# Up-projection with its long and short products in runs of their own, and gate maxima broadcast by DMA instead of by TensorE

## The chip, the cores and the metric

The kernel runs on one core of a Trainium2 chip. The metric is the device time of one execution, in microseconds (us). A core has TensorE (PE, with the weight loads shown as PEld), VectorE (DVE), ScalarE (ACT), GpSimd (POOL) and SyncE (SP, which issues most DMAs). Each engine works through its own instructions in order; semaphores hold an instruction until what it needs is there.

## The reference

One layer of a hybrid block for 256 tokens, width 2048. The parts that matter here are the gates of the chunkwise mLSTM (4 heads, chunks of 128 tokens) and the up-projection of the convolutional feed-forward net:

```python
h = rmsnorm(x, norm1_g[l])
proj = h @ w_in[l]
...
# mLSTM, in each chunk of 128 tokens
b = jnp.cumsum(lf, axis=-1)
dmat = jnp.where(tril, b[..., :, None] - b[..., None, :] + li[..., None, :], -jnp.inf)
inter = b + m_st[..., None]
m_t = jnp.maximum(jnp.max(dmat, axis=-1), inter)
w_in = jnp.exp(dmat - m_t[..., None])
p = jnp.einsum('bhtd,bhsd->bhts', qc, kc) * w_in
...
x = x + y @ w_out[l]
h = rmsnorm(x, norm2_g[l])
u = causal_dwconv(h @ w_up[l], ffn_conv_w[l], ffn_conv_b[l])
u_g, u_v = jnp.split(u, 2, axis=-1)
x = x + (jax.nn.silu(u_g) * u_v) @ w_down[l]
```

`w_up` is 2048 x 11264, `w_down` 5632 x 2048.

## The kernel before

**Weights.** Every weight matrix is streamed once, in chunks of 1 MB. `load_chunk` reads a chunk with one SyncE DMA into `raw` (3 buffers), and for each half of it ScalarE casts the high part `whi` (line 90) and VectorE subtracts to get the low part `wlo` (line 91). Of each there are 4 buffers, one half each, so two chunks. A product with full accuracy is the sum of high times high, high times low and low times high. These steps are given a priority 100 instructions ahead, and a scheduler orders all engines but TensorE by simulated readiness; TensorE keeps the order in which the code is written.

**Stages on TensorE.** First `f_group` (short products of 256 columns, lines 131 to 133: weights stationary, activations `x` moving) for parts of the query and key projections; then `mixer` for each of four heads, made of `t_block` (long products of 512 columns, lines 112 to 114: activations stationary, weights moving), with two more `f_group` stretches in between; then `t_block` for the output projection `w_out`, with the stationary tiles `yh` and `yl`; then the up-projection `wide_group` (lines 610 to 626); then the down-projection (lines 672 to 674, long products).

**Small work in between.** `Slots` counts half chunks: `slots.after(n, fn)` runs `fn` after n of them, so that the gates, the mLSTM and the attention stand between the big products. `gates()` makes rows of 4 heads: `mx`, the running maxima (line 374 completes it). Before, they are split in `mh` and `ml`, and `mlstm` copies row j to all 128 partitions with two products by `selr` and adds the causal mask with a third by `identr`, into the PSUM tile `pm`; ScalarE takes the exponentials from there (line 420). The weights `ptm`, `pth`, `ptl` of the values follow on VectorE and ScalarE, and two half chunks later TensorE multiplies them with the values (lines 437 to 440). The tile `gb` (a gain row, broadcast by a GpSimd DMA) takes over the buffer of `mx`.

**Up-projection.** 22 groups (11 for the gate half into the PSUM tiles `acc`, 11 for the value half into `side`), each of 4 chunks (512 rows of `w_up` by 512 columns). For each of 4 row blocks k and 4 column blocks f there is a pair: a long product, `whi` with the high and low parts of the activations side by side (512 columns), and a short one, `wlo` with the high part alone (256 columns). `spread2` puts four small products into the first group. Behind each group VectorE and ScalarE do the convolution (`ffn_conv`, lines 300 to 308 and 635, 636).

Of the kernel before, what the change touches and what calls it, by code (L numbers as in the profile page):

```python
# [11 lines left out]
F32 = mybir.dt.float32  # L12
F32R = mybir.dt.float32r
AF = mybir.ActivationFunctionType
ALU = mybir.AluOpType
AX = mybir.AxisListType

P = 128
S = 256
# [43 lines left out]
def block_kernel(ctx: ExitStack, tc, x, xT, w_in, ifb, qkw, mg, qg, kg, dl, sg, w_out,  # L63
# [12 lines left out]
    def side():  # L76
        return psum.tile([P, 512], F32, tag="side", name="side")
# [135 lines left out]
    def row_norm(ssq, name):  # L213
# [6 lines left out]
        def spread():  # L220
            ps = side()
            for t in range(2):
# [3 lines left out]
            nc.vector.tensor_copy(rsb, ps[:, :S])  # L226
        return rs, rsb, spread

    sel = start.tile([AH, AH, P], F32, name="sel")
    nc.gpsimd.memset(sel, 0.0)  # L230
    nc.gpsimd.affine_select(sel, sel, pattern=[[-1, AH], [0, P]], compare_op=ALU.not_equal,
                            fill=1.0, base=0, channel_multiplier=1)
    cmask = start.tile([P, P], F32, name="cmask")
    nc.gpsimd.memset(cmask, 0.0)
    nc.gpsimd.affine_select(cmask, cmask, pattern=[[1, P]], compare_op=ALU.is_ge,
                            fill=BIG, base=0, channel_multiplier=-1)
    selr = const.tile([AH, AH, P], F32R, name="selr")
    nc.scalar.copy(selr, sel)
    cmr = const.tile([P, 2, P], F32R, name="cmr")
    nc.scalar.copy(cmr, cmask.unsqueeze(1).broadcast_to([P, 2, P]))  # L240
    identr = const.tile([P, P], F32R, name="identr")
    nc.scalar.copy(identr, ident)

    ifr = const.tile([P, KT, 36], F32, name="ifr")
    nc.gpsimd.memset(ifr, 0.0)
    for n in range(2):
# [81 lines left out]
    def gates():  # L328
# [10 lines left out]
        def rows():  # L339
            ps = side()  # L340
            for k in range(KT):
                a, b = hh[k // 4][:, k % 4], hl[k // 4][:, k % 4]
                w = ws[k // 8][:, k % 8]
                nc.tensor.matmul(ps[:100, :S], w, a, start=k == 0, stop=k == KT - 1, skip_group_check=True)
                nc.tensor.matmul(ps[:36, :S], w[:, :36], b, start=False, stop=k == KT - 1, skip_group_check=True)
            rows4 = pa.tile([AH, 4, S], F32, tag="qn", name="rows4")
            li, f, e, lf = (rows4[:, n] for n in range(4))
            for n, r in enumerate((li, f)):
                nc.scalar.copy(r, ps[64 + 32 * n:64 + 32 * n + AH, :S])
                nc.vector.tensor_tensor(r, ps[32 * n:32 * n + AH, :S], r, ALU.add)  # L350
                nc.vector.tensor_tensor(r, r, rsb1[:AH], ALU.mult)
                nc.vector.tensor_scalar_add(r, r, ib[:, n:n + 1])

            nc.scalar.activation(e, f, AF.Abs)
            nc.scalar.activation(e, e, AF.Exp, scale=-1.0)
            nc.scalar.activation(e, e, AF.Ln, bias=1.0)
            nc.vector.scalar_tensor_tensor(lf, f, 0.0, e, ALU.min, ALU.subtract)

            rows3 = pa.tile([AH, 2 * S + S + P], F32, tag="yb", name="rows3")
            b, nm, a = rows3[:, :S], rows3[:, S:2 * S], rows3[:, 2 * S:]  # L360
            mx = pa.tile([AH, S + P], F32, tag="gb", name="mx", bufs=1)
            for c in range(2):
                cs = slice(c * P, (c + 1) * P)
                nc.vector.tensor_tensor_scan(b[:, cs], ones[:AH, :], lf[:, cs], 0.0, ALU.mult, ALU.add)
            nc.vector.tensor_tensor(a[:, :S], li, b, ALU.subtract)

            nc.vector.tensor_scalar_add(a[:, S:], a[:, :P], b[:, P - 1:P])
            nc.vector.tensor_tensor_scan(mx[:, :P], a[:, :P], a[:, :P], 0.0, ALU.max, ALU.max)
            m1 = pa.tile([AH, 1], F32, name="m1")
            nc.vector.tensor_tensor(m1, b[:, P - 1:P], mx[:, P - 1:P], ALU.add)  # L370
            nc.vector.tensor_tensor_scan(mx[:, P:S], a[:, P:S], a[:, P:S], m1, ALU.max, ALU.max)
            nc.vector.scalar_tensor_tensor(nm, b, -1.0, mx[:, :S], ALU.mult, ALU.subtract)
            nc.vector.tensor_scalar_min(nm, nm, 88.0)
            nc.vector.tensor_copy(mx[:, S:], mx[:, P:S])
            mh = pa.tile([AH, S + P], F32R, name="mh")
            nc.scalar.copy(mh, mx)
            ml = pa.tile([AH, S + P], F32R, name="ml")
            nc.vector.tensor_tensor(ml, mx, mh.bitcast(F32), ALU.subtract)
            gate["mx"] = mh, ml

            def cols():
                pc = side()
                for n, src in enumerate((a[:, :P], a[:, P:S], a[:, S:], nm[:, :P], nm[:, P:])):
                    nc.tensor.transpose(pc[:, n * AH:(n + 1) * AH], src, ident[:AH, :AH])
                ac = pa.tile([P, 3, AH], F32, name="ac")
                em = pa.tile([P, 2, AH], F32, name="em")
                nc.vector.tensor_copy(ac, pc[:, :3 * AH].rearrange("p (n h) -> p n h", h=AH))
                nc.scalar.activation(em, pc[:, 3 * AH:5 * AH].rearrange("p (n h) -> p n h", h=AH), AF.Exp)
                gate["ac"], gate["em"] = ac, em
            slots.after(8, cols)  # L390
# [11 lines left out]
    def mlstm(j, v, hm):  # L402
# [1 line left out]
        gb = pa.tile([P, AV], F32, tag="gb", name="gb", bufs=1)  # L404
        nc.gpsimd.dma_start(gb, mg[:, j * AV:(j + 1) * AV].partition_broadcast(P))
        q, k = qk[j], qk[AH + j]
        pm, pq = side(), side()
        kw = dict(skip_group_check=True)

        for n, mx in enumerate(gate["mx"]):  # L410
            nc.tensor.matmul(pm[:, :3 * P], selr[:, j], mx, start=n == 0, stop=False, **kw)
        nc.tensor.matmul(pm[:, :S], identr, cmr.rearrange("p n s -> p (n s)"), start=False, stop=True, **kw)
        first = pq.rearrange("p (n s) -> p n s", s=S)[:, :, :P]
        for d in range(2):
            nc.tensor.matmul(first, k[:, d, :P], q[:, d], start=d == 0, stop=False, **kw)
# [1 line left out]
        w = pa.tile([P, 3 * P], F32, tag="wt", name="wt", bufs=1)  # L417
        ac = gate["ac"]
        for n in range(3):
            nc.scalar.activation(w[:, n * P:(n + 1) * P], pm[:, n * P:(n + 1) * P], AF.Exp,  # L420
                                 scale=-1.0, bias=ac[:, n, j:j + 1])
        pt = pa.tile([P, 3 * P], F32, tag="ptm", name="ptm", bufs=1)
        nc.vector.scalar_tensor_tensor(pt, pq[:, :3 * P], AQK ** -0.5, w, ALU.mult, ALU.mult)
# [186 lines left out]
    def wide_group(w, col, bank):  # L610


        ps = [bank() for _ in range(4)]
        for c in range(4):
            parts = col_chunk(w, c, col)
            for i in range(2):
                for k in (2 * i, 2 * i + 1):
                    first, last = c == 0 and k == 0, c == 3 and k == 3
                    for f in range(4):
                        whi, wlo = (t[:, f * P:(f + 1) * P] for t in parts[k])  # L620
                        nc.tensor.matmul(ps[f], whi, z[c][:, k].rearrange("p t s -> p (t s)"),  # L621
                                         start=first, stop=last, skip_group_check=True)
                        nc.tensor.matmul(ps[f][:, :S], wlo, z[c][:, k, 0],  # L623
                                         start=False, stop=last, skip_group_check=True)
                slots.tick()
        return ps

# [92 lines left out]
```

## Time and profile before

| | |
|---|---|
| time, median of 3 runs (lowest, highest) | 1592.11 us (1583.66, 1592.16) |
| time of the profiled execution | 1592.0 us |
| its span | 1590.2 us |
| TensorE busy | 1579.3 us (99%) |
| weight loads on TensorE busy | 1340.8 us (84%) |
| VectorE busy | 1112.8 us (70%) |
| ScalarE busy | 827.8 us (52%) |
| GpSimd busy | 35.8 us (2%) |
| granted TensorE clock | 1.00 |
| DMA | 300.88 MB, 189 GB/s mean |

The time of an execution is a little longer than the span of its instructions. Matmuls overlap in the pipeline, so the duration of one on the page is longer than the distance to the next; the distance between starts, which the timeline gives, is what one costs in a stream.

### The profile page before, as it was taken

Reading aid. Unit: us, or ns where it says so; the run is one execution under the profiler, and the core shown is the slowest. Engines: PE = TensorE matmul, PEld = TensorE weight load, DVE = VectorE, ACT = ScalarE, POOL = GpSimd, SP = SyncE. Lnnn points to the kernel's source line nnn. Section 1 sums busy time; section 2 is a strip of 40 time slices with the busy share of each in tenths; the row PEclk is TensorE's granted clock in tenths of the full one; section 3 lists DMA queues with packets and bytes.
Section 4 is the critical chain, followed back from the end, with each engine's and each line's share of the span. In section 5 each row is a group of like instructions: output and inputs, shape, how many; then the busy total and the mean of one; then the engine's idle time right before and its main releaser. Section 6 shows DMA issues by size and latency. Waiting matters only on the chain.

```text
span 1590.2 us, 20513 instructions
## 1 busy us (share of the span) xinstructions
PE 1579.3 (99%) x8021; PEld 1340.8 (84%) x8021; DVE 1112.8 (70%) x1624; ACT 827.8 (52%) x1123; POOL 35.8 (2%) x54
## 2 busy tenths in 40 slices
PE   8999999999999999999999999999999999999998
PEld 8988888888988888888788888888888888888887
DVE  6868676876758757775798777667766776555554
ACT  6854545454554554455455555555555555444442
POOL 0000000000000000000000000000000000000000
PEclk9999999999999999999999999999999999999999
DMA  9656555554645555455655555555555555555553
GB/s 296 225 177 206 171 175 192 172 198 160 209 161 192 185 186 185 159 186 185 238 185 186 186 186 186 186 186 188 186 187 188 187 188 190 193 187 194 202 185 133
DMA packets 138554, 300.88 MB, mean 189 GB/s; under 512 B 9816, under 2 KB 12120, under 8 KB 132312
## 3 DMA queue, kind: packets, MB, share of 16 engines
q1 hardware_dynamic: 137720, 296.41, 55.3%
q10 hardware_dynamic: 416, 2.11, 0.4%
q0 software_dynamic: 320, 1.05, 0.3%
q8 instruction: 63, 1.03, 0.3%
q14 instruction: 35, 0.29, 0.0%
HBM read 297.44 MB, written 2.10 MB: 188 GB/s over the span
## 4 chain that ended last, share of the span: by engine, by line
PE 97%; DVE 1%; DMA 1%; SPq 0%; ACT 0%; issue 0%
PE acc L114 14%; PE acc L112 14%; PE acc L113 14%; PE side L621 10%; PE acc L621 10%; PE acc L623 5%; PE side L623 5%; PE side L674 3%; PE acc L674 3%; PE acc L673 3%; PE side L673 3%; PE acc L672 3%; PE side L672 3%; PE acc L133 2%; PE acc L132 2%; PE acc L131 2%
## 5 line engine op out<-in xcount | busy, mean ns | idle before, releaser
L91 DVE TENSOR_TENSOR wlo<-raw,whi 128x1024 fp32r<-128x1024 f32 x548 | 668.4, 1223 | 363.5 <-ACT whi L90 359.9
L90 ACT CAST whi<-raw 128x1024 fp32r<-128x1024 f32 x548 | 573.9, 1051 | 573.5 <-PE acc L114 234.5
L112 PE MATMUL acc<-whi,x 128*128 128x512 f32 x896 | 352.0, 393 | 0.0
L114 PE MATMUL acc<-whi,x 128*128 128x512 f32 x896 | 349.3, 390 | 0.0
L113 PE MATMUL acc<-wlo,x 128*128 128x512 f32 x896 | 349.0, 390 | 0.0
L621 PE MATMUL side<-x,whi 128*128 128x512 f32 x704 | 249.2, 399 | 0.0
L621 PE MATMUL acc<-x,whi 128*128 128x512 f32 x704 | 249.1, 398 | 0.0
L114 PEld LDWEIGHTS acc<-whi,x 128*128 128x128 f32 x896 | 168.1, 188 | 35.5
L623 PE MATMUL side<-x,wlo 128*128 128x256 f32 x704 | 197.7, 281 | 0.0
L623 PE MATMUL acc<-x,wlo 128*128 128x256 f32 x704 | 197.7, 281 | 0.0
L112 PEld LDWEIGHTS acc<-whi,x 128*128 128x128 f32 x896 | 168.3, 188 | 34.5
L113 PEld LDWEIGHTS acc<-wlo,x 128*128 128x128 f32 x896 | 168.3, 188 | 33.9
L621 PEld LDWEIGHTS side<-x,whi 128*128 128x128 f32 x704 | 132.3, 188 | 33.0
L621 PEld LDWEIGHTS acc<-x,whi 128*128 128x128 f32 x704 | 132.2, 188 | 32.7
L623 PEld LDWEIGHTS acc<-x,wlo 128*128 128x128 f32 x704 | 133.0, 189 | 0.0
L623 PEld LDWEIGHTS side<-x,wlo 128*128 128x128 f32 x704 | 133.0, 189 | 0.0
L308 DVE SCALAR_TENSOR_TENSOR cv<-tu,fwc,cv 128x256 f32<-128x256 f32 x176 | 73.3, 479 | 0.0
L673 PE MATMUL acc<-wlo,ah 128*128 128x512 f32 x176 | 68.5, 389 | 0.0
L672 PE MATMUL acc<-whi,ah 128*128 128x512 f32 x176 | 68.5, 389 | 0.0
L674 PE MATMUL acc<-whi,al 128*128 128x512 f32 x176 | 68.5, 389 | 0.0
L672 PE MATMUL side<-whi,ah 128*128 128x512 f32 x176 | 68.5, 389 | 0.0
L673 PE MATMUL side<-wlo,ah 128*128 128x512 f32 x176 | 68.5, 389 | 0.0
(207 smaller groups left out, 1727.0 us busy)
## 6 DMA issues: line engine op xcount, KB each, us to landing
raw<-w_in SPq DMA_DIRECT2D x126, 1024.0 KB, 5.0
raw<-w_up SPq DMA_DIRECT2D x88, 1024.0 KB, 5.1
raw<-w_down SPq DMA_DIRECT2D x44, 1024.0 KB, 4.8
raw<-w_out SPq DMA_DIRECT2D x16, 1024.0 KB, 5.1
wr<-w_in SPq DMA_DIRECT2D x8, 256.0 KB, 4.4
xs<-x SPq DMA_DIRECT2D x2, 1024.0 KB, 9.4
x<-x ACTq DMA_DIRECT2D x1, 2048.0 KB
out<-x SPq DMA_DIRECT2D x8, 256.0 KB, 2.4
```

The costliest lines, as they stand in the source:

```text
L90: nc.scalar.copy(hi, r)
L91: nc.vector.tensor_tensor(lo, r, hi.bitcast(F32), ALU.subtract)
L112: nc.tensor.matmul(ps[t], ah[c][:, k, tok], whi, start=first, stop=False)
L113: nc.tensor.matmul(ps[t], ah[c][:, k, tok], wlo, start=False, stop=False)
L114: nc.tensor.matmul(ps[t], al[c][:, k, tok], whi, start=False, stop=last)
L131: nc.tensor.matmul(o, whi, ah[c][:, k, :], start=st, stop=False, **kw)
L308: nc.vector.scalar_tensor_tensor(cv[:, f], tu[:, f, 3 - d:3 - d + S], wf[:, j:j + 1], cv[:, f], ALU.mult, ALU.add)
L621: nc.tensor.matmul(ps[f], whi, z[c][:, k].rearrange("p t s -> p (t s)"), start=first, stop=last, skip_group_check=True)
L623: nc.tensor.matmul(ps[f][:, :S], wlo, z[c][:, k, 0], start=False, stop=last, skip_group_check=True)
L672: nc.tensor.matmul(ps[n][t], h_, whi, start=k == 0, stop=False)
L673: nc.tensor.matmul(ps[n][t], h_, wlo, start=False, stop=False)
L674: nc.tensor.matmul(ps[n][t], l_, whi, start=False, stop=k == NFT - 1)
```

## The change

It has two parts. In `wide_group` the pairs are taken apart: in each chunk all 16 long products stand together and all 16 short ones, and the order of the two is reversed from chunk to chunk (`part = (c + i) % 2`), so that chunk 0 ends and chunk 1 begins with short ones, chunk 1 ends and chunk 2 begins with long ones. In the gates `mh`, `ml`, `selr`, `cmr` and `identr` are gone: GpSimd stores `mx` to DRAM, loads it back to all 128 partitions as `mxb`, and writes the causal mask into it with one `affine_select` per head; the exponentials read `mxb`.

```diff
-    sel = start.tile([AH, AH, P], F32, name="sel")
...
-    selr = const.tile([AH, AH, P], F32R, name="selr")
-    nc.scalar.copy(selr, sel)
-    cmr = const.tile([P, 2, P], F32R, name="cmr")
-    nc.scalar.copy(cmr, cmask.unsqueeze(1).broadcast_to([P, 2, P]))
-    identr = const.tile([P, P], F32R, name="identr")
-    nc.scalar.copy(identr, ident)
...
-            mh = pa.tile([AH, S + P], F32R, name="mh")
-            nc.scalar.copy(mh, mx)
-            ml = pa.tile([AH, S + P], F32R, name="ml")
-            nc.vector.tensor_tensor(ml, mx, mh.bitcast(F32), ALU.subtract)
-            gate["mx"] = mh, ml
+            mxd = tc.dram_tile([AH, S + P], F32, name="mxd")
+            nc.gpsimd.dma_start(mxd, mx)
+            mxb = pa.tile([P, AH, S + P], F32, name="mxb")
+            nc.gpsimd.dma_start(mxb, mxd.partition_broadcast(P))
+
+            for j in range(AH):
+                mj = mxb[:, j, :S].rearrange("p (n s) -> p n s", s=P)
+                nc.gpsimd.affine_select(mj, mj, pattern=[[0, 2], [1, P]], compare_op=ALU.is_ge,
+                                        fill=BIG, base=0, channel_multiplier=-1)
+            gate["mx"] = mxb
...
-        pm, pq = side(), side()
+        pq = side()
         kw = dict(skip_group_check=True)
 
-        for n, mx in enumerate(gate["mx"]):
-            nc.tensor.matmul(pm[:, :3 * P], selr[:, j], mx, start=n == 0, stop=False, **kw)
-        nc.tensor.matmul(pm[:, :S], identr, cmr.rearrange("p n s -> p (n s)"), start=False, stop=True, **kw)
...
-            nc.scalar.activation(w[:, n * P:(n + 1) * P], pm[:, n * P:(n + 1) * P], AF.Exp,
+            nc.scalar.activation(w[:, n * P:(n + 1) * P], gate["mx"][:, j, n * P:(n + 1) * P], AF.Exp,
...
             for i in range(2):
-                for k in (2 * i, 2 * i + 1):
-                    first, last = c == 0 and k == 0, c == 3 and k == 3
+                part = (c + i) % 2
+                for k in range(4):
                     for f in range(4):
-                        whi, wlo = (t[:, f * P:(f + 1) * P] for t in parts[k])
-                        nc.tensor.matmul(ps[f], whi, z[c][:, k].rearrange("p t s -> p (t s)"),
-                                         start=first, stop=last, skip_group_check=True)
-                        nc.tensor.matmul(ps[f][:, :S], wlo, z[c][:, k, 0],
-                                         start=False, stop=last, skip_group_check=True)
+                        wt = parts[k][part][:, f * P:(f + 1) * P]
+                        kw = dict(stop=c == 3 and k == 3, skip_group_check=True)
+                        if part == 0:
+                            nc.tensor.matmul(ps[f], wt, z[c][:, k].rearrange("p t s -> p (t s)"),
+                                             start=c == 0 and k == 0, **kw)
+                        else:
+                            nc.tensor.matmul(ps[f][:, :S], wt, z[c][:, k, 0], start=False, **kw)
                 slots.tick()
```

On TensorE, in the first group of the up-projection, the border of the first two chunks stood like this before (`x0` and `x1` are the activations of a chunk, the numbers tell buffers apart):

```order
L621 MATMUL acc_7171<-x0_6627,whi_7179 128x512
L623 MATMUL acc_7171<-x0_6627,wlo_7180 128x256
L621 MATMUL acc_7172<-x0_6627,whi_7179 128x512
L623 MATMUL acc_7172<-x0_6627,wlo_7180 128x256
L621 MATMUL acc_7169<-x1_6797,whi_7217 128x512
L623 MATMUL acc_7169<-x1_6797,wlo_7218 128x256
L621 MATMUL acc_7170<-x1_6797,whi_7217 128x512
L623 MATMUL acc_7170<-x1_6797,wlo_7218 128x256
```

And now the whole first group and the start of the second (16 equal rows are one row with x16; lines 612 and 615 are the long and the short product, line 225 is `spread2`):

```order
L612 MATMUL acc<-x_6609,whi 128x512 x16
L615 MATMUL acc<-x_6609,wlo 128x256 x16
L615 MATMUL acc<-x_6779,wlo 128x256 x16
L612 MATMUL acc<-x_6779,whi 128x512 x16
L612 MATMUL acc<-x_6949,whi 128x512 x16
L615 MATMUL acc<-x_6949,wlo 128x256 x16
L615 MATMUL acc<-x_7119,wlo 128x256 x16
L225 MATMUL side<-diag_7308,ones 128x128
L225 MATMUL side<-diag_7311,ones 128x128
L612 MATMUL acc<-x_7119,whi 128x512 x16
L612 MATMUL side<-x_6609,whi 128x512 x16
```

Long and short alternated from product to product; now they come in runs of 32 (16 at the very start), and a chunk's last high half is used at once with its first.

On ScalarE, around the exponentials of head 0, with the semaphores that each row waits for, it stood like this before:

```order
L388 ACTIVATE em<-side 128x8 [waits DVE_49]
L143 ACTIVATE vh<-acc,rs_577 128x512
L90 CAST whi<-raw 128x1024 [waits DMAHW3_49,PE_49,Activation_49]
L90 CAST whi<-raw 128x1024 [waits PE_49,Activation_49]
L420 ACTIVATE wt<-side,ac 128x128 [waits PE_49]
L420 ACTIVATE wt<-side,ac 128x128 x2
L425 CAST pth<-ptm 128x384 [waits DVE_49]
```

And now:

```order
L379 ACTIVATE em<-side 128x8 [waits DVE_49]
L143 ACTIVATE vh<-acc,rs_561 128x512
L90 CAST whi<-raw 128x1024 [waits DMAHW3_49,PE_49,Activation_49]
L408 ACTIVATE wt<-mxb,ac 128x128 [waits DMASW1_49,Pool_49]
L408 ACTIVATE wt<-mxb,ac 128x128 x2
L90 CAST whi<-raw 128x1024 [waits PE_49,Activation_49]
L413 CAST pth<-ptm 128x384 [waits DVE_49,Activation_49]
```

The exponentials moved ahead of one cast of weights, and they wait for GpSimd and its load (DMASW1) instead of for TensorE.

On GpSimd the mixers' first instructions stood like this before:

```order
L284 AFFINE_SELECT dist<-dist 128x256 [waits Pool_49]
L211 TENSOR_TENSOR rs_577<-rs_577,mhalf 128x2 [waits DVE_49]
L405 DMA gb<-mg 128x512 [waits DMAHW3_49,DMAHW4_49,DMAHW2_49,DMAHW5_49,DMAHW1_49,DMAHW6_49,DMAHW0_49,DMAHW7_49,DVE_49,PE_49]
L211 TENSOR_TENSOR mr<-mr,mhalf 128x1 [waits DVE_49] x2
L405 DMA gb<-mg 128x512 [waits DMASW0_49,DVE_49]
```

And now:

```order
L211 TENSOR_TENSOR rs_561<-rs_561,mhalf 128x2 [waits DVE_49]
L362 DMA mxd<-mx 4x384 [waits DMAHW3_49,DMAHW2_49,DMAHW4_49,DMAHW1_49,DMAHW5_49,DMAHW0_49,DMAHW6_49,DVE_49,DMAHW7_49,PE_49,Activation_49]
L364 DMA mxb<-mxd 128x1536 [waits DMASW0_49]
L396 DMA gb<-mg 128x512
L368 AFFINE_SELECT mxb<-mxb 128x256 [waits DMASW1_49]
L368 AFFINE_SELECT mxb<-mxb 128x256 x3
L211 TENSOR_TENSOR mr<-mr,mhalf 128x1 [waits DVE_49] x2
L396 DMA gb<-mg 128x512 [waits DMASW2_49,DVE_49]
```

The store, the load and four masks stand ahead of the first roots; the load waits for the store's landing (DMASW0), the masks for the load's.

## Rows read from the trace of the kernel before

**Rows 1.** The page: granted clock in 40 slices; chain that ended last, by engine.
```profile
PEclk9999999999999999999999999999999999999999
...
PE 97%; DVE 1%; DMA 1%; SPq 0%; ACT 0%; issue 0%
```

**Rows 2.** Timeline of TensorE, late up-projection (start, duration, engine, line); 33 pairs apart.
```profile
1000.00 0.40 PE L621 MATMUL acc<-x,whi 128*128 128x512 f32 x1
...
1011.66 0.40 PE L621 MATMUL side<-x,whi 128*128 128x512 f32 x1
```

**Rows 3.** Timeline of TensorE, early up-projection; 31 pairs apart.
```profile
854.94 0.39 PE L621 MATMUL acc<-x,whi 128*128 128x512 f32 x1
...
865.69 0.39 PE L621 MATMUL acc<-x,whi 128*128 128x512 f32 x1
```

**Rows 4.** Timeline of TensorE: the products of `spread2`.
```profile
867.77 0.61 PE L225 MATMUL side<-diag,ones 128*128 128x128 f32 x4
```

**Rows 5.** Line 621 on TensorE: count, duration (ns), first and last start.
```profile
L621 PE MATMUL acc<-x,whi x704: 391/398/481, 848.3 to 1322.9; 128*128 128x512 f32 x176
```

**Rows 6.** Timeline of TensorE, `f_group` (short products alone); 99 products apart.
```profile
20.04 0.28 PE L131 MATMUL acc<-x,whi 128*128 128x256 f32 x1
...
31.91 0.28 PE L131 MATMUL acc<-x,whi 128*128 128x256 f32 x1
```

**Rows 7.** Timeline of TensorE, down-projection (long products alone); 52 products apart.
```profile
1400.11 0.39 PE L674 MATMUL side<-whi,al 128*128 128x512 f32 x1
...
1411.90 0.39 PE L672 MATMUL acc<-whi,ah 128*128 128x512 f32 x1
```

**Rows 8.** Timeline of TensorE, output projection (long products alone); 50 products apart.
```profile
800.21 0.40 PE L113 MATMUL acc<-wlo,yh 128*128 128x512 f32 x1
...
811.88 0.40 PE L112 MATMUL acc<-whi,yh 128*128 128x512 f32 x1
```

**Rows 9.** Timeline of TensorE: first and seventh long product behind a short stream.
```profile
430.97 0.40 PE L112 MATMUL acc<-whi,x 128*128 128x512 f32 x1
...
432.36 0.39 PE L112 MATMUL acc<-whi,x 128*128 128x512 f32 x1
```

**Rows 10.** Timelines of ScalarE and VectorE, one half of a chunk.
```profile
1003.97 1.05 ACT L90 CAST whi<-raw 128x1024 fp32r<-128x1024 f32 x1 [1.77 <-PE acc L621]
...
1005.05 1.23 DVE L91 TENSOR_TENSOR wlo<-raw,whi 128x1024 fp32r<-128x1024 f32 x1 [1.60 <-ACT whi L90]
```

**Rows 11.** Timeline of TensorE: last projection product, maxima and first score products of head 0.
```profile
85.70 0.39 PE L114 MATMUL acc<-whi,x 128*128 128x512 f32 x1
86.01 0.43 PE L411 MATMUL side<-mh,selr 4*128 4x384 f32 x1
...
86.78 0.59 PE L415 MATMUL side<-qk 128*128 128x256 f32 x2
```

**Rows 12.** Timelines of VectorE, ScalarE, TensorE: from the maxima to the values of head 0.
```profile
76.60 0.21 DVE L374 COPY mx<-mx 4x128 f32<-4x128 f32 x1
...
87.13 0.88 ACT L420 ACTIVATE wt<-side,ac 128x128 f32<-128x128 f32 x3
...
89.53 0.56 DVE L427 TENSOR_TENSOR ptl<-ptm,pth 128x384 fp32r<-128x384 f32 x1 [0.58 <-ACT pth L425]
...
93.58 0.28 PE L437 MATMUL side<-ones,ptm 128*128 128x1 f32 x2
```

**Rows 13.** DMA issues: transfer, queue, count, KB each, us from issue to landing.
```profile
raw<-w_in SPq DMA_DIRECT2D x126, 1024.0 KB, 5.0
...
xs<-x SPq DMA_DIRECT2D x2, 1024.0 KB, 9.4
...
out<-x SPq DMA_DIRECT2D x8, 256.0 KB, 2.4
...
gb<-mg POOLq DMA_DIRECT2D x4, 256.0 KB, 4.1
```

**Rows 14.** Timeline of GpSimd: a mask of the size of the new ones.
```profile
3.62 0.40 POOL L284 TENSOR_SCALAR_AFFINE_SELECT dist<-dist 128x256 f32<-128x256 f32 x1
```

More of the change, by code (lines that the diff above doesn't have):

```diff
@@ L227, in row_norm @@
         return rs, rsb, spread
-    sel = start.tile([AH, AH, P], F32, name="sel")
[L230 to L236, printed above, removed]
-    selr = const.tile([AH, AH, P], F32R, name="selr")
-    nc.scalar.copy(selr, sel)
-    cmr = const.tile([P, 2, P], F32R, name="cmr")
-    nc.scalar.copy(cmr, cmask.unsqueeze(1).broadcast_to([P, 2, P]))
-    identr = const.tile([P, P], F32R, name="identr")
-    nc.scalar.copy(identr, ident)
     ifr = const.tile([P, KT, 36], F32, name="ifr")
```

## The prediction

> **What bounds the kernel now.** I began with the page. TensorE's clock is granted in full over the whole span, and 97% of the chain of work that ended last is TensorE [rows 1]. So a change moves the time only if it changes what TensorE does per product or makes it stand still. The next question is therefore not how long a product is (its duration on the page overlaps its neighbours) but how far apart two products start. I read that in the timeline of TensorE, from the first and the last start of a long even stretch.
>
> In the up-projection a pair, one long product (512 columns, with the high part of the weights) and one short one (256 columns, with the low part), takes 11.66 us / 33 = 0.3533 us between 1000.00 and 1011.66 [rows 2]. The same pair, with the same operands, took 10.75 / 31 = 0.3468 us between 854.94 and 865.69 [rows 3]. The pace is thus no constant: it changed once, when the four products of `spread2` at 867.77 broke into the stream [rows 4], and it stayed at the slower value to the end of the stage. There are 2 x 704 = 1408 pairs [rows 5]; (867.8 - 848.3) / 0.347 = 56 of them came before the break and 1352 after.
>
> Streams of one kind show what grouping could give. Short products alone, weights stationary and activations moving as in the up-projection, start every 11.87 / 99 = 0.1199 us [rows 6]. Long ones alone start every 11.79 / 52 = 0.2267 us in the down-projection [rows 7], but every 11.67 / 50 = 0.2334 us in the output projection [rows 8]. So there are two paces for long products too, 0.0067 us apart, as the two paces of the pair are.
>
> **The change, part by part.**
>
> *Grouping.* No product is added or dropped; with the new order TensorE meets 16 long and 16 short products per chunk, and because the order reverses from chunk to chunk it meets runs of 32. At the paces of [rows 6, 7] a long and a short cost 0.2267 + 0.1199 = 0.3466 us. Against 0.3533 that is 0.0067 us for each of 1352 pairs: -9.1 us; the 56 pairs that already ran at 0.3468 win nothing. If the long ones run as in [rows 8], the two cost 0.3533 and the gain is nothing. I take the quicker pace because the only other long stream that starts straight behind short products finds it: after the short stream that ends at 430.97, six long products take 432.36 - 430.97 = 1.39 us, 0.03 more than 6 x 0.2267, and behind these the pace is 0.227 [rows 9]. That 0.03 is the price of a switch from short to long. There are 44 such switches (one in every second of 88 chunks): +1.3 us. Net -7.8 us.
>
> *What hides the new order.* A chunk's high parts of both halves are now needed in the first part of an even chunk, and the low parts of both halves at the start of an odd one. The cover is the buffering: 4 halves of each part are two chunks. ScalarE's cast waits for TensorE to free a buffer (1.77 us at 1003.97), takes 1.05 us, and VectorE's subtraction waits for that and takes 1.23 us [rows 10]. A chunk lasts 16 x 0.347 = 5.5 us. In an odd chunk the last high half is freed at its end, and its successor's low part is ready some 1.05 + 1.23 us later, behind up to two more pieces of the convolution of like length on either engine, say 3.5 us; it is needed one chunk (5.5 us) and eight short products (1 us) later. Some 3 us of margin: cost nothing. If that cover goes, the wait falls on TensorE at each border of two groups; that is a rival below.
>
> *Gate maxima.* Three products per head go (two with `selr`, one with `identr`). From the last projection product at 85.70 to the first score product at 86.78 it is 1.08 us [rows 11]; with nothing between, it is one long product, 0.23 us. That saves 0.85 us of TensorE per head, 3.4 us for four. The casts of `selr`, `cmr`, `identr`, `mh` and the subtraction `ml` lie on ScalarE and VectorE while TensorE has work or waits for the first weights: nothing.
>
> *The new wait.* For head 0 the exponentials now wait for a store, a load and GpSimd's first mask, all behind `mx`. In GpSimd's queue the load waits behind the store's landing, and the masks stand behind the load's landing and behind the issue of `gb`; the reciprocal roots queued behind them are wanted only after 93.58. On ScalarE the wait holds up the cast of the next weight half, one place earlier than before. The trace shows neither transfer. `mx` is complete at 76.60 + 0.21 = 76.8 [rows 12]. The store (6 KB): between 2.4 us (256 KB to DRAM) and 4.1 us (`gb`, the same queue) [rows 13]; I take 4.1, the nearest in queue. The load (768 KB): between 4.1 us (256 KB, same queue) and 9.4 us (1 MB beside the start's rush) [rows 13]; I take 5.0 plus one GpSimd issue's worth, 5.7, since 1 MB of weights lands in 5.0. A mask of this size takes 0.40 us [rows 14], four 1.6. So the maxima are masked between 76.8 + 2.4 + 4.1 + 0.4 = 83.7 and 76.8 + 4.1 + 9.4 + 1.6 = 91.9, likeliest 87 to 88.2. TensorE wants the weights of the values at 93.58, now 0.85 earlier, 92.7; from the first exponential at 87.13 to the end of `ptl` at 89.53 + 0.56 it is 3.0 us [rows 12]. The maxima must be there by 89.7. At the likeliest value TensorE doesn't wait; at the worst it stands still 2.2 us, once. I count nothing and keep 2.2 for the range. Later heads read finished data.
>
> The Trainium skill (DMA: Bandwidth & Descriptors, Anatomy of one DMA) puts a GpSimd transfer at about 2.0 us plus bytes over 436 GB/s; by that, an estimate, store and load take 2.0 + 3.8 us, less than I count, and the sum stays the same. The nearest row, `gb`, took 4.1 us where that rule gives 2.6, so it is the row I go by.
>
> **Sum.** Profiled time 1592.0 us (span 1590.2, 1.8 around it), equal to the median of the three runs, 1592.11. 1592.0 - 9.1 + 1.3 - 3.4 = 1580.8 us, 0.7% less. A measurement of this kernel tells about 1% from no change, so this counts as the same.
>
> **Rivals.**
>
> *The order of products doesn't matter* (long products take 0.2334 us in the new runs, as in [rows 8]). For it: that stream, which held its pace with nothing else between, and that the pair's slow pace is exactly 0.2334 + 0.1199. Against it: [rows 3, 7, 9]. Then only the heads are won: 1592.0 - 3.4 = 1588.6 us. The Trainium skill (TensorE: Matmul & The Clock Gate, Back-to-back issue gap) gives for a product apart from others N / 2.4 + 2.5 ns, whatever stands beside it; by that rule too the up-projection wins nothing, and the time would be that same 1588.6. The trace speaks against the rule's number: it would make a pair 325 ns in any order, and [rows 2, 3] show 353 and 347.
>
> *Weights come late (slower than before).* At each of the 22 group borders TensorE waits for a subtraction that is queued behind the convolution on VectorE: one more subtraction, 1.23 us [rows 10], each time: 1580.8 + 27 = 1608 us. It outweighs the gain once the wait passes 11.2 / 22 = 0.51 us per border. For it: in the new order of VectorE two subtractions stand together with seven convolution steps behind them, and buffers are held in another rhythm. Against it: no product of the up-projection waits now, and the margin worked out above is about 3 us.
>
> *Both kinds run slow.* Long at 0.2334 and short at 0.1199 + 0.0067: 1352 x 0.0067 + 56 x 0.0133 - 3.4 = +6.4, 1598.4 us. No short stream in the trace shows that pace.
>
> *Better than the sum.* Inside pairs a short product's successor starts 0.11 to 0.12 us behind it; at 0.117 in runs as well, 1408 x 0.003 = 4.2 us more go: 1576.6 us.
>
> **How the numbers follow.** Forecast 52%; order doesn't matter 23%; weights late 9%; both slow 6%; better 10%. Predicted 1580.8. Its own range, with the 2.2 us of a late load on one side and on the other the 1.3 of the switches and 1 us for what I can't size, is 1578.5 to 1583. The range for 8 in 10 takes in the forecast, the indifferent order (1588.6 plus the 2.2 and another 2 for what I can't size) and the better case (1576.6 less the 1.3 of the switches and another 1.3 for what I can't size): 1574 to 1593. One of the three runs of the kernel before took 1583.66: 1352 x 0.0067 = 9 us less is what it would take if its up-projection kept the pace of [rows 3], so the gain seen may also shrink to 3 us against such a run. Faster by over 1% (under 1576.2) takes the smaller part of the better case and something for what I have not seen: 8%. Slower by over 1% (over 1608) takes half of the late weights and something for what I have not seen: 7%. The same: 85%.
>
> **What would show it.** In the profile after: long products starting 0.227 us apart and short ones 0.120 from the second switch on, the up-projection some 490 us long instead of 497; no idle time before any product of it; a product of `q` and `k` directly behind a projection product, 0.23 us later; `mxb` landed by 87 and the first exponential not later than 89. Wrong if the long products start 0.233 apart, if they stand idle at group borders, or if TensorE stops before the first `ones` product of head 0.

## The result, and the profile after

The kernel after takes 1581.07 us (median of 6 runs, 1580.59 to 1581.57), the kernel before 1592.29 (6 runs, 1583.66 to 1593.04). The ratio is 0.9937 [0.9918, 0.9955]: 0.6% faster, 0.3 us from the forecast of 1580.8, and within the 1% that the forecast counts as the same. (The ratio compares means. The medians are 11.2 us or 0.7% apart; the mean of the kernel before is lower than its median because one of its runs took 1583.66.) The profiled execution took 1581.07 us, with a span of 1579.3 against 1590.2.

The page of the kernel after, granted clock and chain, as in [rows 1]:

```profile
PEclk9999999999999999999999999999999999999999
...
PE 97%; DVE 1%; DMA 1%; SPq 0%; ACT 0%; issue 0%
```

TensorE still sets the end, at full clock. So the question is again where its instructions start. Line 612 (the long product, answering to [rows 5]) and line 663 (first line of the down-projection) of the kernel after: count, duration in ns (lowest, median, highest), first and last start:

```profile
L612 PE MATMUL acc<-x,whi x704: 387/389/496, 845.1 to 1312.5; 128*128 128x512 f32 x176
...
its engine sat idle before it (us, times) until:
  DVE x L583: 0.6, 2
...
L663 PE MATMUL acc<-whi,ah x176: 389/389/397, 1335.0 to 1568.3; 128*128 128x512 f32 x176
```

The first line of the down-projection in the kernel before:

```profile
L672 PE MATMUL acc<-whi,ah x176: 389/389/395, 1345.9 to 1579.2; 128*128 128x512 f32 x176
```

With the 848.3 of [rows 5] the span falls into three pieces. The up-projection starts at 845.1 instead of 848.3, 3.2 us earlier. It lasts 1335.0 - 845.1 = 489.9 us instead of 1345.9 - 848.3 = 497.6, 7.7 less. What is behind it takes 244.3 us in both. Within line 612 nothing waits but the first products, 0.6 us; in the kernel before its line 621 waits for nothing there. The first 16 long products of the stage and the first short one behind them:

```profile
845.07 4.26 PE L612 MATMUL acc<-x,whi 128*128 128x512 f32 x16
849.16 1.12 PE L615 MATMUL acc<-x,wlo 128*128 128x256 f32 x8
```

They take 849.16 - 845.07 = 4.09 us, where 16 at the 0.2267 of [rows 7] would take 3.63: the new order begins the stage some 0.4 us later than it could.

TensorE in the late up-projection of the kernel after, the stretch that answers to [rows 2] (equal products in a row are one line; start, duration of the whole row):

```profile
1005.21 4.00 PE L615 MATMUL side<-x,wlo 128*128 128x256 f32 x32
1009.04 7.44 PE L612 MATMUL side<-x,whi 128*128 128x512 f32 x32
1016.32 4.00 PE L615 MATMUL side<-x,wlo 128*128 128x256 f32 x32
...
1027.44 4.00 PE L615 MATMUL acc<-x,wlo 128*128 128x256 f32 x32
```

32 short products take 1009.04 - 1005.21 = 3.83 us, 0.1197 each, and 32 long ones 7.28 us, 0.2275 each: 11.11 us for 32 pairs, 0.3472 with the switch in it. From 1005.21 to 1027.44 it is 22.23 us for 64, the same, where [rows 2] show 0.3533.

The timeline of TensorE at head 0 in the kernel after answers to [rows 11] and the end of [rows 12]:

```profile
85.86 0.40 PE L114 MATMUL acc<-whi,x 128*128 128x512 f32 x1
86.10 0.60 PE L403 MATMUL side<-qk 128*128 128x256 f32 x2
...
92.90 0.28 PE L425 MATMUL side<-ones,ptm 128*128 128x1 f32 x2
...
93.81 0.39 PE L112 MATMUL acc<-whi,x 128*128 128x512 f32 x1
```

GpSimd of the kernel after, with the store, the broadcast and the masks (in brackets the idle time ahead and what ended it):

```profile
77.79 0.71 POOL L362 DMA_DIRECT2D mxd<-mx  x1 [31.46 <-PE acc L114]
79.94 0.58 POOL L364 DMA_DIRECT2D mxb<-mxd  x1 [1.44 <-DMA mxd<-mx]
...
84.26 2.56 POOL L368 TENSOR_SCALAR_AFFINE_SELECT mxb<-mxb 128x256 f32<-128x256 f32 x4 [3.20 <-DMA mxb<-mxd]
```

ScalarE of the kernel after, the exponentials:

```profile
84.82 0.99 ACT L408 ACTIVATE wt<-mxb,ac 128x128 f32<-128x128 f32 x3
```

The score products follow the projection 0.24 us behind, where it was 1.08, so 0.84 us per head is gone. The maxima have landed by 84.3, the exponentials start at 84.82, 2.3 us earlier than before [rows 12], and the values are multiplied right behind a projection product: no wait.

### The profile page after: what moved, and what is told of

Read it like the earlier page. It is cut to its first block, busy times and chain, and to the rows that moved or that the text cites. A ratio compares the mean times of both kernels' runs of the same rounds, so it can differ in the third digit from the quotient of the medians.

```text
span 1579.3 us, 20483 instructions
## 1 busy us (share of the span) xinstructions
PE 1568.0 (99%) x8009; PEld 1340.7 (85%) x8009; DVE 1104.8 (70%) x1623; ACT 821.9 (52%) x1119; POOL 37.2 (2%) x56
## 4 chain that ended last, share of the span: by engine, by line
PE 97%; DVE 1%; DMA 1%; SPq 0%; ACT 0%; issue 0%; ACTq 0%
PE acc L114 14%; PE acc L113 14%; PE acc L112 14%; PE side L612 10%; PE acc L612 10%; PE side L615 5%; PE acc L615 5%; PE side L665 3%; PE acc L665 3%; PE acc L663 3%; PE side L663 3%; PE acc L664 3%; PE side L664 3%; PE acc L133 2%; PE acc L131 2%; PE acc L132 2%
## 5 line engine op out<-in xcount | busy, mean ns | idle before, releaser
L612 PE MATMUL acc<-x,whi 128*128 128x512 f32 x704 | 166.0, 390 | 0.1
L612 PE MATMUL side<-x,whi 128*128 128x512 f32 x704 | 165.5, 390 | 0.0
L615 PEld LDWEIGHTS side<-x,wlo 128*128 128x128 f32 x704 | 87.4, 192 | 1.7
L615 PEld LDWEIGHTS acc<-x,wlo 128*128 128x128 f32 x704 | 87.4, 192 | 1.7
L615 PE MATMUL side<-x,wlo 128*128 128x256 f32 x704 | 87.9, 283 | 0.0
L615 PE MATMUL acc<-x,wlo 128*128 128x256 f32 x704 | 87.9, 283 | 0.0
```

The costliest lines, as they stand in the source:

```text
L612: nc.tensor.matmul(ps[f], wt, z[c][:, k].rearrange("p t s -> p (t s)"), start=c == 0 and k == 0, **kw)
L615: nc.tensor.matmul(ps[f][:, :S], wt, z[c][:, k, 0], start=False, **kw)
```

## The experiments

No median below gives a ratio that is 1% away from the kernel before. So each is read in us, against the clusters of runs, and from its one profiled execution.

**Each half alone.** `e1_group_only` is the kernel before with the new order in `wide_group`; `e2_gates_only` is the kernel after with the old pairs.

```diff
 e1, against before: wide_group of the kernel after
+                part = (c + i) % 2
+                for k in range(4):
...
 e2, against after: wide_group of the kernel before
+                for k in (2 * i, 2 * i + 1):
...
```

> The kernel before with the grouped order alone; the gates keep their products. Theory (paces): long products start 0.227 us apart and short ones 0.120 in runs of 32, a switch costs about 0.03 us; the up-projection takes some 490 us instead of 497.6, the time is 1592.3 - 7.8 = 1584.5 us. Rival (the order of products is worth nothing, what was won came from the gates or from tiles that moved in memory): 1592 us.

> The changed gates with pairs as before. Theory: three products less per head, 0.85 us each, the up-projection as before with a pair every 0.353 us behind the four products of spread2: 1592.3 - 3.4 = 1588.9 us. Rival (most of the gain is here): 1581 to 1584 us. If the pair should keep its quicker pace of 0.347 us in this program the time would be near 1580, by the pace and not by the gates; the distance of the starts tells which.

The grouping alone took 1584.68 us (12 runs, 1583.93 to 1585.66), ratio 0.9968 [0.9949, 0.9987], the gates alone 1588.95 (9 of 12 runs 1588.43 to 1589.66, three 1580.49 to 1580.78), ratio 0.9991 [0.9969, 1.0014]. From a before of 1592.2 that is -7.5 and -3.2; together -10.7, and both at once gave -11.2: the halves add up to within 0.5 us.

The three quick runs of the gates alone are the case that the expectation names last, and one of them was profiled. TensorE of `e2_gates_only` ahead of `spread2`, behind it, and late in the stage (line 609 is its long product):

```profile
853.95 0.40 PE L609 MATMUL acc<-x,whi 128*128 128x512 f32 x1
...
864.90 0.40 PE L609 MATMUL acc<-x,whi 128*128 128x512 f32 x1
...
865.25 0.61 PE L225 MATMUL side<-diag,ones 128*128 128x128 f32 x4
...
866.04 0.40 PE L609 MATMUL acc<-x,whi 128*128 128x512 f32 x1
...
871.59 0.40 PE L609 MATMUL side<-x,whi 128*128 128x512 f32 x1
...
999.86 0.40 PE L609 MATMUL acc<-x,whi 128*128 128x512 f32 x1
...
1011.99 0.39 PE L609 MATMUL side<-x,whi 128*128 128x512 f32 x1
```

Ahead of the break 31 pairs take 10.95 us, 0.3532 each; behind it 16 take 5.55, 0.3469; and late in the stage 35 take 12.13, 0.3466. That is [rows 2 to 4] the other way round: here the same four products made the pairs quicker.

**Does the break make the pairs slow?** `e5_pairs_unbroken` is the kernel before without the four products; the factors that they spread are set to one, so this part of the computation is left out.

```diff
-    slots.after(7, spread2)
+    slots.after(7, lambda: nc.vector.memset(rsb2, 1.0))
```

> The kernel before without the four products of spread2 in the first group of the up-projection (the row factors of the second norm are set to one, so that part of the computation is left out). Theory (the pair has two paces that hold themselves, and what breaks into the stream decides which): nothing breaks in, the pair keeps 0.347 us to the end, the time is 1592.3 - 9.1 - 0.45 = 1582.8 us. Rival (the slower pace comes with the convolution work that starts behind the first group, or with the tiles in use): 0.353 us from the second group on, 1591.8 us.

8 of 12 runs took 1582.56 to 1583.75 us, four 1591.76 to 1593.03; ratio 0.9994 [0.9970, 1.0018]. In the profiled execution, one of the eight, TensorE late in the up-projection shows:

```profile
999.56 0.39 PE L621 MATMUL acc<-x,whi 128*128 128x512 f32 x1
...
1011.69 0.39 PE L621 MATMUL side<-x,whi 128*128 128x512 f32 x1
```

That is 12.13 us for 35 pairs, 0.3466. So most executions keep the quick pace if nothing breaks in; but a third run as long as the kernel before, with none of the four products to blame (that their pairs are slow is read from the time; none of them was profiled). The kernel before itself has the same two values: of the 85 executions that stood beside all these experiments, 31 took 1583.19 to 1585.78 us and 54 took 1591.65 to 1594.84, none between. What fits all of this: a pace of the pairs is taken up at the entry of the stage, can be changed by a break in either direction, and is otherwise kept. The kernels in which equal products stand in runs of 4, 16 or 32 and nothing else is added (the kernel after, `e1_group_only`, and `e3_runs_of_4`, `e4_no_reversal` and `e8_w_out_tile` below) have one cluster only: the runs of each lie within 1.8 us.

**What a switch costs.** `e3_runs_of_4` puts four long and four short products in a row (352 switches from short to long instead of 44), `e4_no_reversal` doesn't reverse the order (runs of 16, 88 switches).

```diff
 e3
...
-                for k in range(4):
-                    for f in range(4):
-                        wt = parts[k][part][:, f * P:(f + 1) * P]
+                for k in (2 * i, 2 * i + 1):
+                    for part in range(2):
+                        for f in range(4):
+                            wt = parts[k][part][:, f * P:(f + 1) * P]
...
 e4
-                part = (c + i) % 2
+                part = i
```

> The changed kernel, but with 4 long products and then 4 short ones for each row block, so 352 switches from short to long instead of 44. Theory (each switch makes the next four or five long products slower, by 0.015 to 0.03 us together): 308 more switches cost 4.6 to 9 us, 1586 to 1590 us. Rival (only the strict alternation is slow, any run is as good): 1581 us.

> The changed kernel without the reversal: every chunk its 16 long products first, so runs of 16 and 88 switches from short to long instead of 44. Theory: 44 more switches at 0.02 to 0.03 us, 0.9 to 1.3 us, 1582.2 us. Rival (the reversal matters by keeping weights or banks in another rhythm): outside 1580.5 to 1583.5 us, with TensorE idle at chunk borders.

Runs of four: 1586.11 us (12 runs, 1585.76 to 1586.71), ratio 0.9979 [0.9962, 0.9997]. No reversal: 1582.08 (12 runs, 1581.73 to 1583.04), ratio 0.9954 [0.9937, 0.9972]. Against 1581.07 a switch costs 5.04 / 308 = 0.016 us in the one and 1.01 / 44 = 0.023 us in the other. TensorE of `e3_runs_of_4`:

```profile
1000.42 1.09 PE L611 MATMUL acc<-x,whi 128*128 128x512 f32 x4
...
1003.23 1.09 PE L611 MATMUL side<-x,whi 128*128 128x512 f32 x4
1004.16 0.63 PE L614 MATMUL side<-x,wlo 128*128 128x256 f32 x4
1004.63 1.09 PE L611 MATMUL side<-x,whi 128*128 128x512 f32 x4
```

Four long ones take 0.93 us, 0.2325 each, four short ones 0.47, 0.1175: the long ones lose 0.023 in four, and the short ones win 0.010 back. That gain of the short ones is what the step on switches left out.

**How much margin have the weights?** `e6_three_buffers` takes one of the four buffers of `whi` and `wlo` away, in the whole kernel.

```diff
-                hi = wp.tile([P, 1024], F32R, tag="whi", name="whi", bufs=4)
-                lo = wp.tile([P, 1024], F32R, tag="wlo", name="wlo", bufs=4)
+                hi = wp.tile([P, 1024], F32R, tag="whi", name="whi", bufs=3)
+                lo = wp.tile([P, 1024], F32R, tag="wlo", name="wlo", bufs=3)
```

> The changed kernel with 3 instead of 4 buffers for each of the high and low halves. Theory (the margin of some 3 us in weight supply comes from the buffers): a quarter of the cover gone, about 2.8 us of work, TensorE waits little or nothing in the up-projection, below 0.3 us per border of chunks, the time between 1581 and 1590 us. Rival (supply of weights is as tight as one subtraction of 1.23 us): TensorE waits for casts or subtractions in most chunks, 88 x 1 us or more, above 1660 us.

It took 1600.17 us (6 runs, 1598.52 to 1601.76), ratio 1.0067 [1.0042, 1.0092]: between the two theories. The waits of TensorE in this run (us in total, times, longest; the start's first wait left out):

```profile
PE acc L113 <- DVE wlo L91: 2.8, 8, 0.4
...
PE side L664 <- DVE wlo L91: 1.7, 2, 1.0
PE acc L664 <- DVE wlo L91: 1.7, 2, 0.9
...
PE acc L615 <- DVE wlo L91: 0.3, 1, 0.3
```

And of its weight loads, ahead of the up-projection:

```profile
PEld acc L113 <- DVE wlo L91: 10.5, 17, 0.8
```

Only the last of the first rows is in the up-projection, and that lasts from 855.5 to 1346.0, 490.5 us against 489.9. The time is lost in the projections ahead of it, almost all in the mixers (line 113), 10.4 us by 855.5, and at the two ends of the down-projection (lines 663 and 664), 6.4 us. So the stage that the change reorders does with three buffers here; the rest of the kernel needs four.

**What a late broadcast costs.** Extra copies of the 6 KB from DRAM to DRAM stand between the store and the broadcast: four in `e7_longer_broadcast`, then two and three.

```diff
             nc.gpsimd.dma_start(mxd, mx)
+            for n in range(4):
+                mxn = tc.dram_tile([AH, S + P], F32, name=f"mxd{n}")
+                nc.gpsimd.dma_start(mxn, mxd)
+                mxd = mxn
```

> The changed kernel with four more copies of the maxima from DRAM to DRAM ahead of the broadcast. Each copy takes about as long as the store did in the changed kernel, 2.1 us from issue to issue, so the maxima are there some 8.6 us later, at about 93 us. Theory (4 to 5 us of margin): the exponentials start about 93, the values' weights are ready 3.0 us later, TensorE waits for them from 92.9 to 96, about 3 us, and the time is 1584 us. Rival (the wait is hidden anyway because later work fills in): 1581 us. Rival (casts of weights queued behind the exponentials starve TensorE too): 1590 us or more.

It took 1592.63 us (10 runs, 1590.57 to 1594.56), ratio 1.0019 [1.0000, 1.0037]: 11.6 us over the kernel after. The profiled execution, 1590.57, is the shortest of the ten. GpSimd of this run, first and last rows of the chain of copies:

```profile
79.48 0.55 POOL L365 DMA_DIRECT2D mxd<-mxd  x1 [2.26 <-DMA mxd<-mx]
...
93.92 0.56 POOL L368 DMA_DIRECT2D mxb<-mxd  x1 [3.35 <-DMA mxd<-mxd]
98.25 1.49 POOL L372 TENSOR_SCALAR_AFFINE_SELECT mxb<-mxb 128x256 f32<-128x256 f32 x4 [3.77 <-DMA mxb<-mxd]
```

Its TensorE, from the last product ahead of the stop to the seventh long one behind the values:

```profile
92.52 0.39 PE L114 MATMUL acc<-whi,x 128*128 128x512 f32 x1
100.03 0.58 PE L429 MATMUL side<-ones,ptm 128*128 128x1 f32 x2 [7.12 <-DVE ptm L415]
...
102.70 0.63 PE L112 MATMUL acc<-whi,x 128*128 128x512 f32 x1
...
105.00 0.40 PE L112 MATMUL acc<-whi,x 128*128 128x512 f32 x1
```

Its windows ahead of the stop and behind it (stretch, length, busy time of PE, PEld, DVE, ACT and POOL with counts, granted clock, DMA share, GB/s):

```profile
80.00:92.70 12.70, 12.70 (x62) 10.47 (x61) 7.38 (x8) 7.23 (x9) 2.07 (x5) 1.00 0.79 266
...
102.00:104.40 2.40, 2.31 (x6) 1.82 (x6) 0.43 (x4) 0.78 (x2) 0.41 (x1) 0.50 0.65 188
```

A copy took (93.92 - 79.48) / 4 = 3.6 us. TensorE did its projection products until 92.75 and stood still until 100.03, at the products of the values, and for the weights `ptm` alone: 7.3 us. The time is the rival's, but not for its reason: no product waited for a cast of weights, though ScalarE held the casts back. Behind the stop the granted clock is 0.50, TensorE's lower level of 1.2 GHz, until some 104.7 (0.66 on average from 104 to 105). It fell within the stop: it was 1.00 from 95 to 97 and 0.50 from 98 to 100, while TensorE stood still. From the first product of the values to the start at 105.00, six long products further than 102.70, it is 105.00 - 100.03 = 4.97 us; by the kernel after it would be 93.81 - 92.90 = 0.91 to the first long one and 6 x 0.2267 more, 2.27. So the lower clock, with a wait of 0.2 us for `pth` in it, cost another 2.7 us. 7.3 + 2.7 = 10.0, less the 0.15 us by which TensorE had come to this place earlier than in the kernel after, is 9.85; the span is 9.5 us longer, and the 0.35 between them is not traced.

Two and three copies were to tell whether any stop costs the clock.

> Two extra copies instead of four. In the run with four, a copy took (93.92 - 79.48) / 4 = 3.6 us, TensorE stopped at the values of head 0 from 92.75 to 100.03, 1.8 us behind the first mask at 98.25, and then ran at a granted clock of 0.50 until some 104.5, which cost another 2.7 us. Two copies put the first mask at 84.3 + 7.2 = 91.5 and the values at 93.3. Theory A, a late load costs TensorE just the time by which it is late: a stop of about 0.5 us and 1581.6 us. Theory B, whatever the length of the stop the clock falls behind it: 1584.3 us, with a granted clock below 1 right behind 93.

> Three extra copies. The first mask comes at 84.3 + 10.8 = 95.1, the values at 96.9, a stop of TensorE of about 4.1 us from 92.75. Theory A, time for time: 1585.2 us and the clock stays at 1.0. Theory B, the clock falls behind the stop as it did behind 7.3 us: another 2.7 us, 1587.9 us, and a granted clock of 0.50 for some 4 us behind it.

Two copies took 1586.6 us (10 runs, 1584.21 to 1587.96), ratio 0.9985 [0.9964, 1.0007], three 1590.81 (10 runs, 1589.75 to 1591.85), ratio 1.0012 [0.9993, 1.0032]. TensorE around the stop in the run with two:

```profile
92.98 0.39 PE L114 MATMUL acc<-whi,x 128*128 128x512 f32 x1
95.83 0.38 PE L429 MATMUL side<-ones,ptm 128*128 128x1 f32 x2 [2.46 <-DVE ptm L415]
```

A window right behind it:

```profile
96.00:98.00 2.00, 1.84 (x8) 1.28 (x9) 1.25 (x2) 2.00 (x3) 0.00 (x0) 1.00 0.00 0
```

The same two views of the run with three, TensorE first:

```profile
92.62 0.39 PE L114 MATMUL acc<-whi,x 128*128 128x512 f32 x1
99.39 0.59 PE L429 MATMUL side<-ones,ptm 128*128 128x1 f32 x2 [6.38 <-DVE ptm L415]
```

And a window behind that stop:

```profile
102.00:104.00 2.00, 2.00 (x6) 1.61 (x5) 0.64 (x3) 0.60 (x2) 0.58 (x1) 0.50 0.98 356
```

Behind a stop of 2.6 us (93.21 to 95.83) the clock stays at 1.00 and the span is 1582.4, 3.1 over the kernel after: nearly time for time, theory A. Behind one of 6.5 us (92.85 to 99.39) it is 0.50 and the span is 1588.2, 8.9 over: 6.5, and the 2.4 left goes to the clock, theory B. Neither holds for both. The stops were longer than forecast because a copy took anything from 2.2 to 6.1 us (2.2 and 6.1 in the run with two) and, with three, a cast of weights stood between the exponentials. The run behind which the clock stayed up is a single one, the shortest of the ten with two copies. On record are the mean granted clocks of the others too: 0.997 or 0.998 in seven of them, where every run of the kernel after has 0.999 or 1.0. So the clock probably fell in most executions with two copies as well, behind stops that were not profiled; that would fit the 0.9 to 3.8 us by which these seven are longer than the profiled one, but it is argued.

**Why is the output projection slow?** `e8_w_out_tile` puts `yh` and `yl` of three heads into one tile, as the activations of the quick streams are.

```diff
+        if j < 3:
+            both = py.tile([P, 4, 2, S], F32R, name=f"yy{j}")
+            hi, lo = both[:, :, 0], both[:, :, 1]
...
```

> The changed kernel with the high and low parts of the output projection's activations of heads 0 to 2 side by side in one tile, as the mixers' activations lie, instead of in two tiles; head 3's stay in two. Theory (the pace of long products there, 0.2334 us, hangs on where the stationary tiles lie): 0.227 us in three of four chunks, 288 products x 0.0067 = 1.9 us, 1579.2 us. Rival (it is a pace that holds itself, whatever the tiles): 0.2334 us throughout, 1581.1 us.

1581.47 us (10 runs, 1580.55 to 1582.08), ratio 0.9955 [0.9936, 0.9974]: no gain. TensorE in its output projection, 47 products apart:

```profile
800.86 0.40 PE L112 MATMUL acc<-whi,yy 128*128 128x512 f32 x1
...
811.83 0.39 PE L114 MATMUL acc<-whi,yy 128*128 128x512 f32 x1
```

10.97 / 47 = 0.2334, the pace of [rows 8]. That layout of the stationary tiles is not the reason; what is stays open.

## Why the prediction was right

**Grouping, -9.1 us, and 44 switches, +1.3.** Net -7.8 forecast, -7.7 in the profile, but two misses cancel in it. The choice of 0.2267 over the 0.2334 of [rows 8] was right: with it the long products of the kernel after run at 0.2267 from the sixth of a run on, and the rival in which the order of products doesn't matter (1588.6 us) falls with `e1_group_only`. The Trainium skill (TensorE: Matmul & The Clock Gate, Back-to-back issue gap) gives N / 2.4 + 2.5 ns for a product apart from others, by which an estimate is 0.216 and 0.109 us; the trace shows 0.2267 and 0.1197 in runs and 0.3466 or 0.3533 for the two side by side. The same section says that a stream departs from that formula and gives some 131 ns for 512 columns in one, which no run here shows; so the forecast was wrong to take the formula for a rule on streams. The price of a switch, 0.03, was read at one place and for the long side alone; the whole is 0.016 to 0.023, so the 44 cost 0.7 to 1.0 us. The other miss is the wait of the first long products for VectorE's line 583, some 0.4 us: the forecast had no idle time before any product of the stage.

**The reason for the slow pairs** is where a step was wrong without harm. I wrote that the pace changed when `spread2` broke in. `e2_gates_only` shows the same break making it quick, and `e5_pairs_unbroken` slow runs with no break. What the runs support is that the alternating pairs have two paces and the entry or a break decides between them. So grouping does not beat alternation: the quick runs of `e2_gates_only` (1580.5 to 1580.8) are 0.4 us shorter than the kernel after, which is of the size of its switches and of its wait at the start. Grouping holds the pace that alternation has in about a third of the executions of the kernel before. That the profile before, from which the -9.1 was read, and five of the six runs beside the result were of the slow kind was a draw, so the size of the gain is in part luck; the time after does not hang on it. The prediction's remark on the run of 1583.66 fits: against such runs the gain is some 2.7 us.

**Gate maxima, -3.4 us.** -3.2 in the profile: 4 x 0.84 less the 0.16 by which TensorE reached head 0 later (85.86 against 85.70), and -3.2 by `e2_gates_only`. That the casts of the start go for nothing holds.

**Weights late, cost nothing.** Right: line 612 waits for no weights, and `e6_three_buffers` shows the stage 0.6 us longer with a quarter of the cover gone. That the rest of the kernel has less cover than this stage was not asked in the prediction.

**The new wait, cost nothing.** Right in its result, but its three terms were mis-sized. The store's landing took 1.9 us where I took 4.1, the broadcast 4.3 where I took 5.7, the four masks 2.56 where I took 1.6 (they took 1.49 in each of the three runs with copies, so this one is not their usual length). All transfers of the tile `mxd` in the kernel after:

```profile
DMA to landing us min/median/max: 1.9/3.1/4.3
```

The nearest row, `gb`, was the wrong one to size a transfer of 6 KB by. The Trainium skill (DMA: Bandwidth & Descriptors, Anatomy of one DMA) would have given, as an estimate, 2.0 and 3.8 us; the trace agrees for the store and is 0.5 over for the broadcast. The price at the bad end, 2.2 us once, is of the right kind by `e9_two_copies`. Beyond that end it would have been too low: a stop of 6.5 us cost 2.4 more for the clock. The limit of 89.7 was too strict: it asked for `ptl`, but the first products of the values start once `ptm` is there, 1.8 us behind the masks' start in `e7_longer_broadcast`, so some 91.

**The margin.** The sum came out 0.3 us from the median: -10.9 in the span against -11.2, the 0.1 of the grouping and the 0.2 of the gates. That it is so small is luck in part: the switches cost 0.3 to 0.6 us less than forecast and the start of the stage 0.4 more.

## What to carry to other kernels

Before a stream of products is reordered, read the distance of their starts at several places and in several executions: a stream that alternates long and short products can have two paces, and one profile shows only one draw of it. A product on the bounding engine that only copies or masks a few rows can go to an idle engine and the DMA, if the chain is priced with each landing and set against the moment at which the result is wanted, several us ahead of it. And if such a chain comes late, look at the granted clock behind the stop: a long one costs more than its own length.

## What the runs showed of the hardware

- Products come at steps: 0.2267 or 0.2334 us (512 columns), 0.1197 (256 columns), 0.3466 or 0.3533 for both in turn. In the profile before, the pace of the pairs held from `spread2` to the end of the stage, some 470 us. What picks it was not found.
- Behind short products it takes long ones about five to reach their pace (in the kernel after they start at 429.44, 429.68, 429.91, 430.14, 430.37, 430.61, and from there on 0.2267 apart); in a run of four they stand at 0.2325, and the short ones behind them at 0.1175.
- TensorE's granted clock was 0.50 behind stops of 6.5 and 7.3 us, and 1.00 behind one of 2.6 us, in one profiled execution each.
- One of the four new masks on GpSimd took 1.47 us in the kernel after, the others 0.41; in the runs with copies four took 1.49. Copies of 6 KB from DRAM to DRAM took 2.2 to 6.1 us from issue to issue, beside the same weight stream.
